# SwiGLU half steps by seven products of quarters: sums of products kept in PSUM chains, and operand sums moved from GpSimd to VectorE

## The chip, the cores and the metric

The kernel runs on one core of one Trainium2 chip. The metric is the device time of one execution in microseconds (us). The engines are called TensorE (PE in the rows; PEld is its weight load), VectorE (DVE), ScalarE (ACT), GpSimd (POOL) and SyncE (SP, which issues the DMAs here).

## What is computed

One step of a hybrid block for 128 prompt tokens and 512 sample tokens: a SwiGLU half step, a mixer (a gated delta rule and attention), a second SwiGLU half step, and the final norm. D_MODEL is 1024, D_FF is 2816. The change concerns the two half steps:

```python
def modulate(x, shift, scale):
    return x * (1 + scale) + shift

def swiglu(h, w13, w2):
    a, b = jnp.split(h @ w13, 2, axis=-1)
    return (jax.nn.silu(a) * b) @ w2

def ffn_sublayer(x, norm_w, shift, scale, gate, w13, w2):
    return x + HALF_STEP * gate * swiglu(modulate(rms_norm(x, norm_w), shift, scale), w13, w2)

xp = ffn_sublayer(xp, norm_ffn1[l], sh1p, sc1p, g1p, ffn1_w13[l], ffn1_w2[l])
...
xs = ffn_sublayer(xs, norm_ffn1[l], sh1s, sc1s, g1s, ffn1_w13[l], ffn1_w2[l])
```

## The kernel before

Features lie on the 128 partitions and the 640 tokens (prompt and samples together) on the free axis, in two halves of 320. Every product is made from exact parts of float32 operands (a first part and a rest, called hi and lo), by three matmuls: hi x hi, hi x lo, lo x hi. `parts` makes them: ScalarE casts the hi part (L128: wh for 1024 columns, sh for 512), VectorE subtracts it for the lo part (L132: wl, sl). The weights come by DMA into three buffers called wraw.

A half step (`ffn`, L475) walks over 22 feature tiles of 128 in rounds of 4, 4, 3, 3, 4 and 4; after each round the projection with w2 adds the round's tiles to the residual. The first three tiles are direct products (`product`, L144), whose silu(a) * b is made at L491 and L492 (tile s). The other 19 of each half step, 38 in the kernel, are pairs (`product_pair`, L567): a and b of one feature tile, each split into quarters (two halves of k by two halves of the tokens), are made by seven products P1 to P7 instead of eight, by Winograd's form of Strassen's algorithm. A product of quarters is 12 matmuls of 128x128 by 128x320 (`products`, L200, matmul in L207).

For this the operands are combined. `combined_operands` (L527) sums the hi and lo parts of the token quarters on GpSimd (L536, 12 for each half step), makes T1, T2 and T3 from them on VectorE (L541) and splits them again (L545 on VectorE). `last_operand` (L550) does the same for T4: 8 sums on GpSimd (L558), then VectorE (L562, L564). In every pair, GpSimd makes four sums of weights f[0] to f[3] (L577 to L580, tile ss, four buffers), which `parts` splits. The end of the direct products and the first pairs are called a transition below; in the profiled execution they lie at 51 to 99 us and 1158 to 1203 us.

In a pair the seven products go in the order P1, P6, P5, P7, P2, P3, P4. Each of P1, P6, P5, P7 and P4 has a PSUM bank of its own out of a ring of four (aux), P2 and P3 share a tile of two banks (big, a ring of two). ScalarE copies P1 (L590). Then VectorE adds and multiplies:

```python
        nc.vector.tensor_tensor(u[:, 0], s[:, 0], p6, op=ALU.add)
...
        nc.vector.tensor_tensor(u[:, 0], u[:, 0], p7, op=ALU.add)
        nc.vector.tensor_tensor(u[:, 1], s[:, 1], p7, op=ALU.add)
...
        nc.vector.tensor_tensor(s, s, both[:, :, 0:HT], op=ALU.add)
        nc.scalar.activation(s, s, AF.Silu)
...
        nc.vector.tensor_tensor(s[:, 1], s[:, 1], u[:, 1], op=ALU.mult)
        nc.vector.tensor_tensor(u[:, 0], u[:, 0], p4, op=ALU.add)
        nc.vector.tensor_tensor(s[:, 0], s[:, 0], u[:, 0], op=ALU.mult)
```

They stand at L593, L596, L599, L600, L604 (both banks of big, 640 columns), L605 (silu, 640 columns), L608, L609 and L610. At the end of each tile ScalarE casts the result (gh, L501) and VectorE makes its rest (gl, L502). The order of the instructions on each engine is set by a scheduler from the order of the program, its priorities and the buffers; each engine then runs its queue in order.

Of the kernel before, what the change touches and what calls it, by code (L numbers as in the profile page):

```python
# [10 lines left out]
F32 = mybir.dt.float32  # L11
# [3 lines left out]
AF = mybir.ActivationFunctionType  # L15
# [4 lines left out]
P = 128  # L20
# [75 lines left out]
# columns of a half (0: the prompt and the first 192 samples, 1: samples alone) by kind, 0 prompt, 1 sample  # L96
# [3 lines left out]
class Net:  # L100
# [9 lines left out]
    # ---------------------------------------------------------------- weights  # L110
# [8 lines left out]
    def parts(self, raw, small=False):  # L119
        """Exact split of float32 weights into two float32r parts."""  # L120
# [23 lines left out]
    def product(self, w, xs, c0=0, split=None):  # L144
        """[128 features, tokens] = w^T x over the k tiles; operands come as exact parts. split: None for one
        view of both halves, otherwise a view of each half, in small tiles when true."""
# [38 lines left out]
    def products_by_half(self, ws, xs, done):  # L185
        """Several products with the second halves of all before the first ones; done(i, half, psum)."""
# [13 lines left out]
    def products(self, ps, w, xs):  # L200
        """One half of the tokens and of the k tiles: ps (+)= w^T x."""
        nc = self.nc
        wh, wl = w
        n = len(xs)
        for k, (xh, xl) in enumerate(xs):
            for j, (wt, xt) in enumerate(((wh, xh), (wh, xl), (wl, xh))):
                nc.tensor.matmul(  # L207
                    ps,
                    lhsT=wt[:, k * P : (k + 1) * P],
                    rhs=xt,  # L210
                    start=(k == 0 and j == 0),
                    stop=(k == n - 1 and j == 2),
                )

    # ---------------------------------------------------------------- small helpers
    def rsqrt(self, y, x):
        """y = x ** -0.5, elementwise on a small tile."""
# [14 lines left out]
    # ---------------------------------------------------------------- setup  # L232
# [37 lines left out]
    def modulation(self, m):  # L270
        """One of the nine modulation vectors, features on partitions, for prompt and sample; a generator with one
        quarter of the k tiles in each step."""
# [34 lines left out]
    def modulation_part(self, m0, g):  # L307
        """Two feature tiles (2 g, 2 g + 1) of the modulation vectors m0 and m0 + 1."""
# [35 lines left out]
    def scale_columns(self, m, at, t, d0=0, n=KD):  # L344
        """norm weight * (1 + scale) as per-partition columns."""
# [9 lines left out]
    def token_rstd(self, ss):  # L355
        """[128 tokens, n] sums of squares -> rstd."""
# [8 lines left out]
    def half_rstd(self, acc, h):  # L365
        """rstd of the tokens of one half, from squares [128, 2, 320]: columns of 128 tokens that start at 0, 128
        and 192, so the last one overlaps."""
# [8 lines left out]
    def half_rows(self, columns):  # L376
        """(column of 128 tokens, first token, tokens, place) -> a row [320] on each partition."""
# [19 lines left out]
    def modulated(self, hs, X, rb, A, m_shift, h, ds):  # L397
        """x * rstd * A + shift of one half as two exact parts, for the feature tiles ds."""
# [23 lines left out]
    def next_operands(self, last, X, A, m_shift):  # L422
        """Operands of the next products; last: the generator that makes the last tiles of X."""
# [14 lines left out]
    def add_square(self, acc, x, first):  # L438
        """acc (+)= x * x for one half."""
# [15 lines left out]
    def residual(self, ws, xs, X, gate, tail, weight=None):  # L455
        """X += gate * product, with the squares of the sums gathered in acc; the last tiles go by halves."""
# [18 lines left out]
    # ---------------------------------------------------------------- ffn  # L475
    def ffn(self, hs, X, gate, w13, w2, gpool, between=None, first=(), weight=None):
        """X += gate * swiglu(h); squares of the result are gathered into acc."""
# [49 lines left out]
    def combined_operands(self, hs):  # L527
        """The parts of the sums of quarters of h = [[B11, B12], [B21, B22]] (k halves by token halves) that
        product_pair takes: T1 = B12 - B11, T2 = B22 - T1, T3 = B22 - B12."""
        nc = self.nc  # L530
        T = [[], [], []]
        for d in range(KH):
            v = []
            for k, h in ((d, 1), (d, 0), (d + KH, 1)):
                t = self.tile(self.phase, [P, HT], F32, "ht", self.nht)
                nc.gpsimd.tensor_tensor(t, *(x[:, h, :].bitcast(F32) for x in hs[k]), op=ALU.add)  # L536
# [13 lines left out]
    def last_operand(self, hs, B):  # L550
        """B21 - T2, in the place of B12."""
        nc = self.nc
        B["T4"] = []
        for d in range(KH):
            v = []
            for x in (B["21"][d], B["T2"][d]):
                t = self.tile(self.phase, [P, HT], F32, "ht", self.nht)
                nc.gpsimd.tensor_tensor(t, x[0].bitcast(F32), x[1].bitcast(F32), op=ALU.add)  # L558
# [8 lines left out]
    def product_pair(self, w, ca, cb, B, s):  # L567
        """s = silu(a) * b for the products a, b of two tiles of features with h, by seven products of quarters
        in place of eight (Winograd's form of Strassen's product)."""
# [13 lines left out]
        for i in (1, 0, 2, 3):  # L583
            S[i] = self.parts(f[i], True)
        b22 = self.parts(b[:, n:], True)
        u = self.tile(self.phase, [P, 2, HT], F32, "u", self.nu)
        bank = lambda: self.aux_tile()[:, 0:HT]
        p1 = bank()
        self.products(p1, (ha[:, :n], la[:, :n]), B["11"])
        nc.scalar.copy(s[:, 0], p1)  # L590
        p6 = bank()
        self.products(p6, S[1], B["T2"])
        nc.vector.tensor_tensor(u[:, 0], s[:, 0], p6, op=ALU.add)  # L593
        p5 = bank()
        self.products(p5, S[0], B["T1"])
        nc.vector.tensor_tensor(s[:, 1], u[:, 0], p5, op=ALU.add)  # L596
        p7 = bank()
        self.products(p7, S[2], B["T3"])
        nc.vector.tensor_tensor(u[:, 0], u[:, 0], p7, op=ALU.add)  # L599
        nc.vector.tensor_tensor(u[:, 1], s[:, 1], p7, op=ALU.add)  # L600
        both = self.tile(self.big, [P, 2, 512], F32, "big", 2)
        self.products(both[:, 0, 0:HT], (ha[:, n:], la[:, n:]), B["21"])
        self.products(both[:, 1, 0:HT], S[3], B["22"])
# [1007 lines left out]
```

## Time and profile before

| | |
|---|---|
| three runs | 1602.48, 1606.65, 1610.18 us (median 1606.65) |
| profiled execution, span from first to last instruction | 1605.0 us (no time of its own is listed beside the span) |
| TensorE busy | 1542.7 us (96%) |
| VectorE busy | 1100.8 us (69%) |
| ScalarE busy | 664.5 us (41%) |
| GpSimd busy | 368.7 us (23%) |
| mean granted TensorE clock | 0.989 of full speed |
| first half step, mixer, second half step, output | about 51 to 500, 500 to 1137, 1137 to 1588, 1588 to 1605 us |

The busy share of an engine is an average over stages with different limits. The lists of waits name for each engine what it waited for last, and the timeline shows single instructions with their start and duration. A matmul's duration (0.31 us) is longer than the step from one to the next, as matmuls overlap in the engine.

### The profile page before, as it was taken

Reading aid. Unit: us, or ns where it says so; the run is one execution under the profiler, and the core shown is the slowest. Engines: PE = TensorE matmul, PEld = TensorE weight load, DVE = VectorE, ACT = ScalarE, POOL = GpSimd, SP = SyncE. Lnnn points to the kernel's source line nnn. Section 1 sums busy time; section 2 is a strip of 40 time slices with the busy share of each in tenths; the row PEclk is TensorE's granted clock in tenths of the full one; section 3 lists DMA queues with packets and bytes.
Section 4 is the critical chain, followed back from the end, with each engine's and each line's share of the span. In section 5 each row is a group of like instructions: output and inputs, shape, how many; then the busy total and the mean of one; then the engine's idle time right before and its main releaser. Section 6 shows DMA issues by size and latency. Waiting matters only on the chain.

```text
span 1605.0 us, 28532 instructions
## 1 busy us (share of the span) xinstructions
PE 1542.7 (96%) x11242; PEld 1457.5 (91%) x11242; DVE 1100.8 (69%) x2241; ACT 664.5 (41%) x1234; POOL 368.7 (23%) x306
## 2 busy tenths in 40 slices
PE   6989999999999899999899999999879999999998
PEld 4889999999999798788899999899879999999997
DVE  5866666668576768886665655764796766767675
ACT  4433323324243646554455544333542424334244
POOL 3632131222220220100221213000352232331310
PEclk8999999999999999999999999999999999999999
DMA  9444434545325241214533324545022322323122
GB/s 329 148 144 141 159 123 143 163 152 168 119 82 137 82 138 44 65 40 134 161 117 94 98 78 127 158 127 167 14 79 79 92 66 66 106 66 106 53 79 66
DMA packets 221296, 181.17 MB, mean 113 GB/s; under 512 B 16160, under 2 KB 198621, under 8 KB 221163
## 3 DMA queue, kind: packets, MB, share of 16 engines
q1 hardware_dynamic: 220907, 179.29, 36.3%
q8 instruction: 89, 1.46, 0.4%
q14 instruction: 44, 0.36, 0.1%
q0 software_dynamic: 256, 0.06, 0.0%
HBM read 161.59 MB, written 16.42 MB: 111 GB/s over the span
## 4 chain that ended last, share of the span: by engine, by line
PE 80%; DVE 11%; issue 3%; ACT 2%; DMA 2%; POOL 2%; SPq 0%; POOLq 0%; DVEq 0%; ACTq 0%
PE big L177 29%; PE aux L207 20%; PE aux L177 9%; PE aux L164 9%; PE big L207 8%; DVE ht L404 1%; DVE wl L132 1%; PE aux L281 1%; DVE ht L541 1%; DVE sl L132 1%; PE aux L161 1%; DMA wraw<-ffn_w 1%; DVE x L451 1%; DVE tl L545 1%; DVE cacc L867 1%
## 5 line engine op out<-in xcount | busy, mean ns | idle before, releaser
L128 ACT CAST wh<-wraw 128x1024 fp32r<-128x1024 f32 (+1 forms) x147 | 150.8, 1026 | 266.3 <-PE aux L177 90.1
L132 DVE TENSOR_TENSOR wl<-wraw,wh 128x1024 fp32r<-128x1024 f32 (+1 forms) x145 | 181.8, 1254 | 85.7 <-ACT wh L128 84.4
L177 PE MATMUL big<-hl,wh 128*128 128x320 f32 x768 | 194.7, 321 | 6.9 <-POOL hl L411 4.3
L177 PE MATMUL big<-hh,wh 128*128 128x320 f32 x768 | 187.8, 319 | 4.0 <-ACT hh L1293 1.8
L177 PE MATMUL big<-hh,wl 128*128 128x320 f32 x768 | 187.8, 315 | 0.7 <-DVE wl L132 0.7
L128 ACT CAST sh<-ss 128x512 fp32r<-128x512 f32 x152 | 92.5, 620 | 185.1 <-POOL ss L578 93.6
L577 POOL TENSOR_TENSOR ss<-wraw 128x512 f32<-128x512 f32 x38 | 53.9, 1418 | 485.0 <-DMA wraw<-ffn_w 337.3
L132 DVE TENSOR_TENSOR sl<-ss,sh 128x512 fp32r<-128x512 f32 x152 | 132.3, 880 | 46.8 <-ACT sh L128 45.9
L207 PE MATMUL aux<-th,sh 128*128 128x320 f32 x456 | 141.3, 310 | 3.2 <-DVE s L492 2.8
L177 PEld LDWEIGHTS big<-hl,wh 128*128 128x128 f32 x768 | 131.4, 190 | 13.0 <-POOL hl L411 7.0
L207 PE MATMUL aux<-tl,sh 128*128 128x320 f32 x456 | 141.1, 309 | 0.0
L207 PE MATMUL aux<-th,sl 128*128 128x320 f32 x456 | 140.8, 309 | 0.0
L177 PEld LDWEIGHTS big<-hh,wh 128*128 128x128 f32 x768 | 129.0, 190 | 9.8 <-issue 3.1
L177 PEld LDWEIGHTS big<-hh,wl 128*128 128x128 f32 x768 | 131.1, 190 | 5.8 <-issue 4.6
L451 DVE SCALAR_TENSOR_TENSOR x<-big,gate,x 128x128 f32<-128x128 f32 (+2 forms) x181 | 67.4, 422 | 34.6 <-PE big L177 34.3
L177 PE MATMUL big<-gh,wh 128*128 128x320 f32 x352 | 88.7, 313 | 1.1 <-ACT gh L501 1.1
L207 PEld LDWEIGHTS aux<-th,sh 128*128 128x128 f32 x456 | 85.8, 188 | 4.0 <-DVE s L492 3.0
L177 PE MATMUL big<-gl,wh 128*128 128x320 f32 x352 | 87.6, 310 | 0.0
L177 PE MATMUL big<-gh,wl 128*128 128x320 f32 x352 | 87.0, 308 | 0.0
L207 PEld LDWEIGHTS aux<-tl,sh 128*128 128x128 f32 x456 | 85.7, 188 | 0.0
L207 PEld LDWEIGHTS aux<-th,sl 128*128 128x128 f32 x456 | 85.7, 188 | 0.0
L1055 DVE TENSOR_TENSOR P<-aux,lv 128x512 f16<-128x512 f32 x70 | 48.2, 688 | 49.1 <-PE aux L164 49.1
(373 smaller groups left out, 4014.0 us busy)
## 6 DMA issues: line engine op xcount, KB each, us to landing
wraw<-ffn_w SPq DMA_DIRECT2D x116, 512.0 KB, 3.9
araw<-ada_w SPq DMA_DIRECT2D x56, 512.0 KB, 5.8
wraw<-w_in SPq DMA_DIRECT2D x35, 512.0 KB, 3.8
araw<-ada_w SPq DMA_DIRECT2D x32, 256.0 KB, 6.5
wraw<-ffn_w SPq DMA_DIRECT2D x16, 384.0 KB, 3.1
gd<-stage SPq DMA_DIRECT2D x16, 320.0 KB, 2.9
wraw<-w_out SPq DMA_DIRECT2D x8, 512.0 KB, 4.3
xd<-x SPq DMA_DIRECT2D x8, 320.0 KB, 2.2
```

Of the source, the lines that this page charges most:

```text
L128: nc.scalar.copy(hi, raw)
L132: nc.vector.tensor_sub(lo, raw, hi.bitcast(F32))
L161: self.marks.append(self.nc.tensor.transpose(*args))
L164: self.marks.append(self.nc.tensor.matmul(*args, **kw))
L177: self.nc.tensor.matmul(ps[h], lhsT=wt[:, k, c0 : c0 + P], rhs=xt[:, h, :], start=(k == 0 and j == 0), stop=(k == len(xs) - 1 and j == 2),)
L207: nc.tensor.matmul(ps, lhsT=wt[:, k * P : (k + 1) * P], rhs=xt, start=(k == 0 and j == 0), stop=(k == n - 1 and j == 2),)
L281: nc.tensor.matmul(ps[32 * g : 32 * g + 32], lhsT=self.s32[:, k, :], rhs=raw[:, g * 256 : (g + 1) * 256], start=(k % 2 == 0), stop=(k % 2 ...
L404: mark = nc.vector.scalar_tensor_tensor(t[:, cols], X[d][:, h, cols], A[:, d, v : v + 1], rb[:, cols], op0=ALU.mult, op1=ALU.mult)
L451: nc.vector.scalar_tensor_tensor(X[:, h, cols], ps[:, cols], gate[:, d, v : v + 1], X[:, h, cols], op0=ALU.mult, op1=ALU.add)
L541: nc.vector.tensor_sub(f[i], v[x], v[y] if y < 3 else f[0])
L577: nc.gpsimd.tensor_tensor(f[0], b[:, :n], b[:, n:], op=ALU.add)
L1055: nc.vector.tensor_tensor(P16, p1, mask, op=ALU.mult)
```

## The change

`products` gets an argument `start`; without it, the product is added to what its bank holds. In `product_pair` the products go in the order P1, P5, P6, P3, P7, P2, P4. P1, P6, P7 and P4 add up in one bank (`chain`, the first of a big tile), P5 and P3 in another (`side`, an aux bank); P2 has the second bank of the big tile. ScalarE copies the chain after P1 (c1), the side after P5 (c5) and the chain after P6 (c6); VectorE makes five operations instead of eight, and the silu goes by halves. The weight sums are split in the order 0, 1, 3, 2. The sums of L536 and L558 go to VectorE. Lines of the changed kernel behind `products` are one higher than before; the changed line numbers of the pair are L593, L596, L599 (the copies c1, c5, c6), L601 (s1), L603 (c5 + chain), L604 (silu), L606 (s0), L608, L609 (silu) and L610. The diff also takes out comments, which are left out here.

```diff
-    def products(self, ps, w, xs):
+    def products(self, ps, w, xs, start=True):
...
-                    start=(k == 0 and j == 0),
+                    start=(start and k == 0 and j == 0),
                     stop=(k == n - 1 and j == 2),
+                    skip_group_check=not start,
...
     def combined_operands(self, hs):
...
-                nc.gpsimd.tensor_tensor(t, *(x[:, h, :].bitcast(F32) for x in hs[k]), op=ALU.add)
+                nc.vector.tensor_tensor(t, *(x[:, h, :].bitcast(F32) for x in hs[k]), op=ALU.add)
...
     def last_operand(self, hs, B):
...
-                nc.gpsimd.tensor_tensor(t, x[0].bitcast(F32), x[1].bitcast(F32), op=ALU.add)
+                nc.vector.tensor_tensor(t, x[0].bitcast(F32), x[1].bitcast(F32), op=ALU.add)
...
     def product_pair(self, w, ca, cb, B, s):
...
-        for i in (1, 0, 2, 3):
+        for i in (0, 1, 3, 2):
             S[i] = self.parts(f[i], True)
         b22 = self.parts(b[:, n:], True)
-        u = self.tile(self.phase, [P, 2, HT], F32, "u", self.nu)
-        bank = lambda: self.aux_tile()[:, 0:HT]
-        p1 = bank()
-        self.products(p1, (ha[:, :n], la[:, :n]), B["11"])
-        nc.scalar.copy(s[:, 0], p1)
-        p6 = bank()
-        self.products(p6, S[1], B["T2"])
-        nc.vector.tensor_tensor(u[:, 0], s[:, 0], p6, op=ALU.add)
-        p5 = bank()
-        self.products(p5, S[0], B["T1"])
-        nc.vector.tensor_tensor(s[:, 1], u[:, 0], p5, op=ALU.add)
-        p7 = bank()
-        self.products(p7, S[2], B["T3"])
-        nc.vector.tensor_tensor(u[:, 0], u[:, 0], p7, op=ALU.add)
-        nc.vector.tensor_tensor(u[:, 1], s[:, 1], p7, op=ALU.add)
         both = self.tile(self.big, [P, 2, 512], F32, "big", 2)
-        self.products(both[:, 0, 0:HT], (ha[:, n:], la[:, n:]), B["21"])
-        self.products(both[:, 1, 0:HT], S[3], B["22"])
-        nc.vector.tensor_tensor(s, s, both[:, :, 0:HT], op=ALU.add)
-        nc.scalar.activation(s, s, AF.Silu)
-        p4 = bank()
-        self.products(p4, b22, B["T4"])
-        nc.vector.tensor_tensor(s[:, 1], s[:, 1], u[:, 1], op=ALU.mult)
-        nc.vector.tensor_tensor(u[:, 0], u[:, 0], p4, op=ALU.add)
-        nc.vector.tensor_tensor(s[:, 0], s[:, 0], u[:, 0], op=ALU.mult)
+        chain, p2 = both[:, 0, 0:HT], both[:, 1, 0:HT]
+        side = self.aux_tile()[:, 0:HT]
+        kept = lambda: self.tile(self.phase, [P, HT], F32, "ht", self.nht)
+        self.products(chain, (ha[:, :n], la[:, :n]), B["11"])
+        c1 = kept()
+        nc.scalar.copy(c1, chain)
+        self.products(side, S[0], B["T1"])
+        c5 = kept()
+        nc.scalar.copy(c5, side)
+        self.products(chain, S[1], B["T2"], start=False)
+        c6 = kept()
+        nc.scalar.copy(c6, chain)
+        self.products(side, S[3], B["22"], start=False)
+        nc.vector.tensor_tensor(s[:, 1], c6, side, op=ALU.add)
+        self.products(chain, S[2], B["T3"], start=False)
+        nc.vector.tensor_tensor(c5, c5, chain, op=ALU.add)
+        nc.scalar.activation(s[:, 1], s[:, 1], AF.Silu)
+        self.products(p2, (ha[:, n:], la[:, n:]), B["21"])
+        nc.vector.tensor_tensor(s[:, 0], c1, p2, op=ALU.add)
+        self.products(chain, b22, B["T4"], start=False)
+        nc.vector.tensor_tensor(s[:, 1], s[:, 1], c5, op=ALU.mult)
+        nc.scalar.activation(s[:, 0], s[:, 0], AF.Silu)
+        nc.vector.tensor_tensor(s[:, 0], s[:, 0], chain, op=ALU.mult)
```

The change also moves instructions. Three places matter; the names are tiles, with a number of their buffer or version.

On TensorE, in a pair of the fifth round of the second half step, before: the end of P7 (its own bank, aux) and the start of P2 (big).

```order
L207 MATMUL aux_16538<-th_13510,sh_16483 128x320
L207 MATMUL aux_16538<-tl_13511,sh_16483 128x320
L207 MATMUL aux_16538<-th_13510,sl_16484 128x320
L207 MATMUL big_16553<-hh_12512,wh_16471 128x320 [waits PE_49]
L207 MATMUL big_16553<-hl_12513,wh_16471 128x320
L207 MATMUL big_16553<-hh_12512,wl_16472 128x320
```

The same place after the change: the end of P7 (the chain in big_16431), five matmuls of the next pair's P1 (big_16573), and the start of P2, which is in the tile of the chain.

```order
L207 MATMUL big_16431<-tl_13473,sh_16423 128x320
L207 MATMUL big_16431<-th_13472,sl_16424 128x320
L207 MATMUL big_16573<-hh_12466,wh_16549 128x320 [waits DVE_49]
L207 MATMUL big_16573<-hl_12467,wh_16549 128x320
L207 MATMUL big_16573<-hh_12466,wl_16550 128x320
L207 MATMUL big_16573<-hh_12468,wh_16549 128x320
L207 MATMUL big_16573<-hl_12469,wh_16549 128x320
L207 MATMUL big_16431<-hh_12474,wh_16407 128x320 [waits DVE_49]
L207 MATMUL big_16431<-hl_12475,wh_16407 128x320
```

P2 followed P7 directly and waited for no reader of P7. Now five matmuls of the next P1 stand between, and P2 waits for VectorE: for L603, which reads the chain. P4 stands in the same way behind L606 and five more such matmuls.

On ScalarE, in the second pair of that round, before: the copy of P1 (L590), casts of the pair before (gh) and of the weight sums (sh), and the cast of a weight that is being loaded for the pair after the next (wh).

```order
L590 COPY s_16314<-aux_16352 128x320
L501 CAST gh_16168<-s_16170 128x320
L128 CAST sh_16475<-ss_16464 128x512
L128 CAST wh_16615<-wraw_16603 128x1024
L128 CAST sh_16479<-ss_16463 128x512
L128 CAST sh_16483<-ss_16465 128x512
L128 CAST sh_16487<-ss_16466 128x512
```

The same place after the change, with the copies c1 (L593), c5 (L596) and c6 (L599).

```order
L593 COPY ht_16303<-big_16289 128x320
L502 CAST gh_16108<-s_16110 128x320
L128 CAST wh_16549<-wraw_16537 128x1024
L128 CAST sh_16411<-ss_16399 128x512
L596 COPY ht_16317<-aux_16290 128x320
L128 CAST sh_16415<-ss_16400 128x512
L599 COPY ht_16331<-big_16289 128x320
L128 CAST sh_16419<-ss_16402 128x512
```

The cast wh stood behind the only copy of the pair. Now it stands ahead of c5 and c6, for which the products P3 and P7 wait.

On VectorE, at the start of the first half step's transition, before: the first operations on the combined operands (ht, tl) and on two weights (wl).

```order
L132 TENSOR_TENSOR wl_659<-wraw_656,wh_658 128x1024
L541 TENSOR_TENSOR ht_777<-ht_771,ht_773 128x320
L541 TENSOR_TENSOR ht_779<-ht_775,ht_771 128x320
L132 TENSOR_TENSOR wl_714<-wraw_711,wh_713 128x1024
L541 TENSOR_TENSOR ht_781<-ht_775,ht_777 128x320
L545 TENSOR_TENSOR tl_784<-ht_777,th_783 128x320
```

The same place after the change.

```order
L537 TENSOR_TENSOR ht_771<-hh_209,hl_210 128x320
L537 TENSOR_TENSOR ht_773<-hh_209,hl_210 128x320
L132 TENSOR_TENSOR wl_659<-wraw_656,wh_658 128x1024
L537 TENSOR_TENSOR ht_775<-hh_217,hl_218 128x320
L132 TENSOR_TENSOR wl_714<-wraw_711,wh_713 128x1024
L542 TENSOR_TENSOR ht_777<-ht_771,ht_773 128x320
L542 TENSOR_TENSOR ht_779<-ht_775,ht_771 128x320
L542 TENSOR_TENSOR ht_781<-ht_775,ht_777 128x320
L546 TENSOR_TENSOR tl_784<-ht_777,th_783 128x320
```

The sums of the hi and lo parts (L537, GpSimd's L536 before) now stand in VectorE's own queue ahead of the differences of L542 (L541 before) that take them.

## Rows read from the trace of the kernel before

**Rows 1.** The page, its first part: busy us, share of the span, number of instructions of each engine.

```profile
PE 1542.7 (96%) x11242; PEld 1457.5 (91%) x11242; DVE 1100.8 (69%) x2241; ACT 664.5 (41%) x1234; POOL 368.7 (23%) x306
```

**Rows 2.** By stretch: length, busy PE, PEld, DVE, ACT, POOL; granted clock, DMA share, GB/s.

```profile
51.00:99.00 48.00, 40.23 (x281) 36.74 (x284) 40.90 (x56) 19.11 (x38) 32.18 (x25) 0.93 0.43 143
1158.00:1203.00 45.00, 36.94 (x237) 36.09 (x236) 43.22 (x55) 21.26 (x41) 28.71 (x25) 0.92 0.23 71
...
1210.00:1400.00 190.00, 190.00 (x1293) 189.34 (x1292) 132.78 (x234) 68.90 (x109) 56.31 (x40) 1.00 0.27 81
```

**Rows 3.** What TensorE waited for: line and what released it, us, times, longest.

```profile
PE aux L177 <- DVE s L492: 5.9, 1, 5.9
...
PE aux L207 <- DVE wl L132: 4.6, 1, 4.6
...
PE aux L207 <- DVE s L492: 2.8, 1, 2.8
```

**Rows 4.** The same view by stretch as rows 2, behind two long waits of TensorE.

```profile
89.00:95.50 6.50, 6.42 (x27) 6.42 (x28) 6.04 (x12) 4.08 (x9) 0.35 (x1) 0.58 0.41 126
1193.90:1197.00 3.10, 3.10 (x13) 3.10 (x13) 3.10 (x5) 0.62 (x2) 1.42 (x2) 0.51 0.53 169
```

**Rows 5.** TensorE in order of time: start, duration; first and last matmul of a P1.

```profile
1445.20 0.31 PE L207 MATMUL aux<-hh,wh 128*128 128x320 f32 x1
...
1446.81 0.31 PE L207 MATMUL aux<-hh,wl 128*128 128x320 f32 x1
```

**Rows 6.** Groups by line and shape: busy us, mean ns | idle before, releaser.

```profile
L541 DVE TENSOR_TENSOR ht<-ht,ht 128x320 f32<-128x320 f32 x24 | 20.7, 906 | 4.5 <-POOL ht L536 4.5
L545 DVE TENSOR_TENSOR tl<-ht,th 128x320 fp32r<-128x320 f32 x24 | 20.4, 874 | 0.1
L593 DVE TENSOR_TENSOR u<-s,aux 128x320 f32<-128x320 f32 x38 | 18.4, 485 | 27.5 <-PE aux L207 26.8 <-ACT s L590 0.6
```

**Rows 7.** VectorE and GpSimd in order of time in the first half step's transition.

```profile
66.91 1.97 DVE L541 TENSOR_TENSOR ht<-ht,ht 128x320 f32<-128x320 f32 x3 [1.28 <-POOL ht L536]
68.80 3.35 DVE L545 TENSOR_TENSOR tl<-ht,th 128x320 fp32r<-128x320 f32 x3
...
68.55 3.24 POOL L536 TENSOR_TENSOR ht<-hh,hl 128x320 f32<-128x320 f32 x3 [0.84 <-DVE ht L541]
```

**Rows 8.** VectorE, ScalarE and GpSimd in order of time around one pair.

```profile
1454.77 0.47 DVE L599 TENSOR_TENSOR u<-u,aux 128x320 f32<-128x320 f32 x1
1455.16 0.47 DVE L600 TENSOR_TENSOR u<-s,aux 128x320 f32<-128x320 f32 x1
...
1447.16 0.43 ACT L590 COPY s<-aux 128x320 f32<-128x320 f32 x1 [0.85 <-PE aux L207]
...
1450.84 1.05 ACT L128 CAST wh<-wraw 128x1024 fp32r<-128x1024 f32 x1 [1.40 <-DMA wraw<-ffn_w]
1451.79 1.17 ACT L128 CAST sh<-ss 128x512 fp32r<-128x512 f32 x2
...
1445.48 1.49 POOL L580 TENSOR_TENSOR ss<-wraw,ss 128x512 f32<-128x512 f32 x1 [0.69 <-DVE sl L132]
```

**Rows 9.** Groups by line and shape as in rows 6.

```profile
L608 DVE TENSOR_TENSOR s<-s,u 128x320 f32<-128x320 f32 x38 | 21.6, 569 | 7.8 <-ACT s L605 7.8
...
L590 ACT COPY s<-aux 128x320 f32<-128x320 f32 x38 | 16.2, 426 | 36.1 <-PE aux L207 28.5 <-DVE gl L502 7.6
```

**Rows 10.** VectorE, then TensorE in order of time, end of a wait for L492.

```profile
1200.76 0.88 DVE L492 TENSOR_TENSOR s<-s,aux 128x320 f32<-128x320 f32 x2
...
1201.30 0.42 PE L207 MATMUL aux<-th,sh 128*128 128x320 f32 x1 [2.75 <-DVE s L492]
1201.55 0.31 PE L207 MATMUL aux<-tl,sh 128*128 128x320 f32 x1
```

**Rows 11.** The page, its sixth part: DMA issues, KB each, us from issue to landing.

```profile
wraw<-ffn_w SPq DMA_DIRECT2D x116, 512.0 KB, 3.9
```

**Rows 12.** The instructions of L608: least, median and largest duration in ns.

```profile
L608 DVE TENSOR_TENSOR s<-s,u x38: 478/492/1519, 112.6 to 1559.9; 128x320 f32<-128x320 f32 x38
```

## The prediction

> **What bounds the kernel now.** I read the profile from the whole to the part. The busy shares come first: TensorE is busy for 96% of the span and nobody else for more than 69% [rows 1], so the time can only change where TensorE's work changes or where it waits. The number of matmuls doesn't change. The windows by stage come next [rows 2]: through the steady part of the second half step TensorE is busy for 190.0 of 190 us at full clock, while around the two transitions (direct products to products of quarters) it is busy for only 40.2 of 48 and 36.9 of 45 us, at a mean clock of 0.93 and 0.92. There VectorE is busy for 40.9 of 48 and 43.2 of 45 us and GpSimd for 32.2 and 28.7 us. Then TensorE's list of waits [rows 3] names those stalls: 5.9 us and 2.8 us for an s of L492, 4.6 us for a wl. After the two long ones it runs at half clock, 1.2 GHz: 27 matmuls in 6.5 us and 13 in 3.1 us [rows 4]. At full clock 11 steps of a product take 1.61 us, so one takes 0.147 us [rows 5]; the half clock has cost 6.5 - 27 x 0.147 = 2.5 and 3.1 - 13 x 0.147 = 1.2 us. All that can come back is therefore 5.9 + 2.5 = **8.4 us** in the first half step and 4.6 + 2.8 + 1.2 = **8.6 us** in the second. In the 38 pairs there is nothing to win, since TensorE doesn't wait in them, but something to lose.
>
> **The sums that move to VectorE (gain).** The 24 additions of L541 take 0.906 us and the 24 of L545 0.874 us, although the same shape with an operand in PSUM (L593) takes 0.485 us [rows 6]. The timeline shows why: they run long beside GpSimd's L536 and come to an end with it [rows 7]. The Trainium skill (SBUF — State Buffer, section "Who interferes with whom") says that a VectorE instruction with two SBUF inputs and a GpSimd one that reads SBUF exclude each other for a whole instruction; by that rule, the trace agrees. The excess of the two groups is 24 x 0.42 + 24 x 0.39 = 19.5 us, about 9.7 in each half step, and VectorE also waits 4.5 us for L536. What is added is 20 sums in each half step, one every 0.40 us (a 0.47 to 0.49 us instruction starts 0.39 us before the next one, L599 to L600 [rows 8]): 8.0 us. In the first half step VectorE has 7 of 48 us idle besides, mostly waits for GpSimd, so the late s comes early enough: I take all **8.4 us**, and none if its queue is still late. In the second it is idle for under 2 of 45 us, the net relief is some 2 us in these two groups and perhaps 5 more in the sl, wl and gl that GpSimd held up too: I take **6.4** of 8.6, with bounds 1 and 8.6. Sum: -14.8 us (bounds -1 and -17).
>
> **The chains (loss).** Before, each product had its own PSUM bank, and its reader could be late without harm: in the pair shown P7, the fourth product, ended near 1445.20 + 47 x 0.147 + 0.31 = 1452.4, and L599 read it at 1454.77 [rows 5, 8]. Now four products go to one tile, and the next matmul on it waits until it was read. The removed VectorE work (8 additions and multiplications a pair down to 5) and the two more copies and one more silu on ScalarE (a copy is 0.43 us [rows 9]) lie beside TensorE; I cost them at nothing while those queues keep up.
>
> 1. P2 waits for VectorE's L603 and P4 for L606, each with five matmuls of another product before it. From the start of the last matmul of P7 the fillers give 6 x 0.147 = 0.88 us. The way round needs 0.31 (the matmul) + 0.04 (end of a matmul at 1447.12 to the copy at 1447.16 [rows 5, 8]) + 0.48 (the addition) + 0.06 (an s that ends at 1201.24 to the matmul at 1201.30 [rows 10]) = 0.89 us. It comes 0.01 us late, and after any wait the second matmul starts 0.25 instead of 0.147 us behind the first [rows 10], so each costs 0.115 us. For 38 pairs: 2 x 38 x 0.115 = **8.7 us** (bounds 0, if five matmuls are just enough, and 12). The Trainium skill (PSUM — Partial Sum Buffer, section "PSUM bank collisions raise a hardware error") asks for such guards by bank. P2 writes another bank than the one that L603 reads; by that rule its wait wouldn't be needed and the sum would be 4.4 us lower. The program's order has the wait, as the tile of two banks is guarded as one, so I keep 8.7.
>
> 2. ScalarE works in order, and the cast of a weight that must first be loaded (wh) now stands ahead of the copy c5. In the pair shown wh began at 1450.84, after 1.40 us of waiting for its load; the load follows GpSimd's last sum of the pair before, which ended at 1446.97, by 3.9 us [rows 8, 11]. P1 began at 1445.20, so P3, which needs c5, is due 36 x 0.147 = 5.3 us later, at 1450.5. c5 would come behind wh (0.95) and one sh (0.52): 1450.84 + 0.95 + 0.52 + 0.43 + 0.06 = 1452.8, 2.3 us late. GpSimd's sum had waited 0.69 us for an sl [rows 8], which the shorter VectorE queue may give back: I take 1.6. The next pair is itself later by that and I take 1.1 there; the first and last pair of a round have no such load ahead: 2.7 us for each of three rounds of four pairs. In the two rounds of three the wh of the projection stands ahead of c1 instead; without the sh it is 1.8 late by the same rows, and I take 1.6. Second half step: 3 x 2.7 + 2 x 1.6 = **11.3 us** (bounds 0, if loads start earlier, and 3 x 4.6 + 2 x 1.8 = 17).
>
> 3. In the first half step wh stands ahead of c1 or of no copy in most pairs: **2 us** (0 to 10).
>
> 4. VectorE's L608, ahead of the L606 that P4 needs, takes 0.492 us in the median but up to 1.519 us beside GpSimd, 0.09 us over its least on average (0.569 against 0.478 [rows 9, 12]): 38 x 0.09 = **3.4 us** (0 to 16, below).
>
> Loss: 8.7 + 11.3 + 2 + 3.4 = 25.4 us. Sum: 1605.0 - 14.8 + 25.4 = 1615.6 us against the profiled execution, whose span is 1605.0 us. The median of the three runs is 1606.65, 1.65 us more: **1617 us**. The mixer keeps its order and counts for nothing.
>
> **The rivals.**
> - *The bridges hold, faster.* Five matmuls are just enough and the loads come early, since the load chain hangs on GpSimd, which has lost 40 sums. What is left of the loss is some 3 us; all 17 us come back: 1606.65 - 17 + 3 = 1593 us. For it: the way round misses by only 0.01 us. Against it: the wait of 1.40 us for a load [rows 8] is there although GpSimd had long been idle. It decides at the point where c5 ends before 36 matmuls of its pair have gone.
> - *Only the loads cost, same.* Bridges hold (-8.7) and the rest stays: 1617 - 9 = 1608 us.
> - *GpSimd's sums fall into the round trips, slower still.* If they meet L608 or the gl behind it in half of the pairs, for the 1.0 us that the worst L608 shows, the loss grows by 19 x 1.0 - 3.4 = 16: 1633 us. The skill's rule on exclusion, named above, makes this the worst case for each pair. Against it: the median L608 isn't slowed [rows 12].
> - *VectorE is still late at the transitions.* The 40 sums that it takes on cost 16 us of its time, nearly as much as the 19.5 us won. Then only some 4 of the 14.8 us come back: 1628 us.
>
> **How the numbers follow.** Forecast 0.38 (1617, own range 1609 to 1625). Bridges hold 0.23 (1593). Only the loads 0.20 (1608). GpSimd in the round trips 0.09, VectorE late 0.10. The measurement tells 0.5%, about 8 us, from no change: under 1598.6 is faster, over 1614.7 slower. Faster: 0.23 and a little of the second rival, 0.26. Slower: two thirds of the forecast, 0.25, and both late cases, 0.19, together 0.44. Same: the rest, 0.30. The range leaves out the lower half of the first rival and the end of the late cases: 1593 to 1632 us.
>
> **What would show it.** Right: the waits for s of L492 and for wl at the transitions are gone and the clock there is near 1.0; in the pairs new waits appear on TensorE for L603 and L606 of some 0.1 us each and for copies c1 and c5 of 1 to 2 us in the middle pairs of a round, with ScalarE waiting for a load ahead. Wrong: no wait over 0.3 us within the pairs (the first rival), or stalls at the transitions as long as before, or clock lost in the steady stretch, which nothing above counts.

## The result and the profile after

The changed kernel takes 1634.77 us in the median of its executions, the kernel before 1606.65 us: the ratio is 1.0165, with an interval of 1.0145 to 1.0184. The prediction was 1617 us with a range to 1632, so the direction was right and the size was not: by the ratio 27 us were lost where 10 were forecast. One execution, of 3283.83 us, in which the matmuls of pairs took some 0.55 us each in place of 0.31, is left out of the ratio, and its cause is open. The profile below is that of a later execution of the same kernel (the first experiment).

The first part of the page, which answers to [rows 1], and the windows, which answer to [rows 2]:

```profile
PE 1562.3 (96%) x11242; PEld 1459.7 (90%) x11242; DVE 1061.3 (65%) x2167; ACT 696.0 (43%) x1348; POOL 336.1 (21%) x266
```

```profile
51.00:99.00 48.00, 44.45 (x332) 40.61 (x331) 39.20 (x77) 20.04 (x42) 8.72 (x4) 1.00 0.54 170
1158.00:1203.00 45.00, 40.05 (x256) 38.72 (x255) 41.39 (x88) 26.92 (x57) 10.27 (x8) 0.96 0.18 53
...
1210.00:1400.00 190.00, 183.81 (x1230) 180.42 (x1230) 122.38 (x197) 69.66 (x123) 59.09 (x40) 1.00 0.26 77
```

TensorE has the same number of matmuls and the span is 25 us longer. TensorE's busy time is 20 us longer too (1542.7 before), so much of the loss lies in matmuls that take longer, and no list of waits shows that part. In the window of the first transition it is busy for 44.5 instead of 40.2 us, in that of the second for 40.1 instead of 36.9, and the granted clock there rose from 0.93 and 0.92 to 1.00 and 0.96. GpSimd has fallen from 32.2 to 8.7 us. So the transitions have won, as forecast. The steady stretch, in which TensorE was busy for all of 190 us, now has 183.8.

TensorE's list of waits, which answers to [rows 3]:

```profile
PE big L207 <- DVE s L606: 13.5, 13, 2.5
...
PE aux L177 <- DVE wl L132: 3.7, 1, 3.7
PE big L207 <- ACT ht L593: 3.6, 7, 1.3
...
PE aux L207 <- ACT ht L596: 0.6, 1, 0.6
```

The waits of 5.9 and 2.8 us for s are gone; one of 3.7 us for a wl is left at the second transition. New are 13.5 us in 13 places for L606, the addition that P4 waits for, and 4.2 us for the copies c1 (L593) and c5 (L596). One pair of the second half step, on VectorE, ScalarE, GpSimd and TensorE in order of time (start, duration):

```profile
1251.78 0.49 DVE L603 TENSOR_TENSOR ht<-ht,big 128x320 f32<-128x320 f32 x1
1252.34 1.22 DVE L132 TENSOR_TENSOR sl<-ss,sh 128x512 fp32r<-128x512 f32 x1
1253.49 0.48 DVE L608 TENSOR_TENSOR s<-s,ht 128x320 f32<-128x320 f32 x1
1254.49 0.98 DVE L503 TENSOR_TENSOR gl<-s,gh 128x320 fp32r<-128x320 f32 x1 [0.52 <-ACT gh L502]
1255.39 0.48 DVE L606 TENSOR_TENSOR s<-ht,big 128x320 f32<-128x320 f32 x1
```

```profile
1254.00 0.46 ACT L502 CAST gh<-s 128x320 fp32r<-128x320 f32 x1 [1.69 <-DVE s L608]
```

```profile
1251.72 1.29 POOL L580 TENSOR_TENSOR ss<-wraw,wraw 128x512 f32<-128x512 f32 x1 [0.63 <-DVE sl L132]
1253.71 1.42 POOL L581 TENSOR_TENSOR ss<-wraw,ss 128x512 f32<-128x512 f32 x1 [0.69 <-DVE sl L132]
```

```profile
1252.32 0.42 PE L207 MATMUL big<-hh,wh 128*128 128x320 f32 x1
1252.58 0.32 PE L207 MATMUL big<-hl,wh 128*128 128x320 f32 x1
...
1254.06 0.46 PE L207 MATMUL big<-hh,wl 128*128 128x320 f32 x2
...
1255.92 0.41 PE L207 MATMUL big<-hh,sh 128*128 128x320 f32 x1 [0.83 <-DVE s L606]
```

P2 starts at 1252.32 and its last matmul at 1254.06, so L606 could have read it near 1254.4. It starts at 1255.39. Ahead of it in VectorE's queue stand an sl of 1.22 us, L608, and a gl that first waits for ScalarE's gh and then takes 0.98 us; sl and gl run beside two sums of GpSimd, and in the median of the trace they take 0.69 and 0.49 us. TensorE stands idle for 0.83 us ahead of P4 for that alone. P2's own wait, for L603, costs what the prediction said: its second matmul comes 0.26 us behind its first.

### The profile page after: what moved, and what is told of

It is laid out like the page before. It is cut to its first block, busy times and chain, and to the rows that moved or that the text cites. A ratio compares the mean times of both kernels' runs of the same rounds, so it can differ in the third digit from the quotient of the medians.

```text
span 3282.1 us, 28408 instructions
## 1 busy us (share of the span) xinstructions
PE 3266.0 (100%) x11242; PEld 2945.3 (90%) x11242; DVE 1019.2 (31%) x2167; ACT 708.5 (22%) x1348; POOL 302.9 (9%) x266
## 4 chain that ended last, share of the span: by engine, by line
PE 99%; DVE 0%; issue 0%; DMA 0%; ACT 0%; SPq 0%; DVEq 0%; ACTq 0%
PE big L177 38%; PE big L207 23%; PE aux L177 14%; PE aux L207 9%; PE aux L164 9%; PE aux L282 3%; PE aux L161 1%; PE aux L323 1%; PE aux L1344 0%; PE aux L1250 0%; PE aux L382 0%; PE aux L883 0%; PE aux L1239 0%; PE aux L372 0%; PE big L1396 0%
## 5 line engine op out<-in xcount | busy, mean ns | idle before, releaser
L177 PE MATMUL big<-hl,wh 128*128 128x320 f32 x768 | 334.7, 526 | 0.9 <-DVE hl L417 0.6
L177 PE MATMUL big<-hh,wl 128*128 128x320 f32 x768 | 327.5, 516 | 0.0
L177 PE MATMUL big<-hh,wh 128*128 128x320 f32 x768 | 326.9, 522 | 0.1
L177 PEld LDWEIGHTS big<-hh,wl 128*128 128x128 f32 x768 | 233.9, 319 | 15.0 <-issue 8.3
L177 PEld LDWEIGHTS big<-hh,wh 128*128 128x128 f32 x768 | 230.9, 317 | 17.5 <-issue 6.3
L177 PEld LDWEIGHTS big<-hl,wh 128*128 128x128 f32 x768 | 232.9, 319 | 10.9 <-issue 2.2
L207 PE MATMUL big<-th,sh 128*128 128x320 f32 x304 | 168.4, 554 | 0.0
L207 PE MATMUL big<-th,sl 128*128 128x320 f32 x304 | 168.3, 554 | 0.0
L207 PE MATMUL big<-hl,wh 128*128 128x320 f32 x304 | 167.8, 552 | 0.0
L207 PE MATMUL big<-tl,sh 128*128 128x320 f32 x304 | 167.6, 551 | 0.0
L177 PE MATMUL big<-gh,wl 128*128 128x320 f32 x352 | 166.3, 554 | 0.0
L207 PE MATMUL big<-hh,wl 128*128 128x320 f32 x304 | 165.2, 555 | 0.0
L207 PE MATMUL big<-hh,wh 128*128 128x320 f32 x304 | 164.9, 542 | 0.0
L207 PEld LDWEIGHTS big<-hh,wh 128*128 128x128 f32 x304 | 99.4, 327 | 34.4 <-issue 15.8
```

The source lines that it names most:

```text
L177: self.nc.tensor.matmul(ps[h], lhsT=wt[:, k, c0 : c0 + P], rhs=xt[:, h, :], start=(k == 0 and j == 0), stop=(k == len(xs) - 1 and j == 2),)
L207: nc.tensor.matmul(ps, lhsT=wt[:, k * P : (k + 1) * P], rhs=xt, start=(start and k == 0 and j == 0), stop=(k == n - 1 and j == 2), skip_gr ...
```

## The experiments

All times are compared with runs of the kernel before on the same chip; differences in us are made from the ratios and 1606.8 us. A ratio's interval is 2 to 5 us wide to either side, so differences of a few us between two runs aren't clear of noise.

**The change again.** No edit.

> The changed kernel itself, for a profile that can be read beside that of before and a second interval. Every theory expects 1630 to 1636 us, some 27 us more than before. The prediction's account (transitions win 15 us, waits in the pairs cost 25) must be off by 17 us somewhere: if the transitions didn't win, the stalls behind s of L492 (L493 now) and wl are still there with 4 us and more; if the pairs cost more, TensorE's new waits in the 38 pairs add up to some 42 us, and the list of waits says which of L603, L606 and the copies carry them.

Measured: 1635.79 us, ratio 1.0181 [1.0162, 1.0199]. The profile is the one above.

**The sums alone.** The kernel before, with the sums of L536 and L558 on VectorE:

```diff
-                nc.gpsimd.tensor_tensor(t, *(x[:, h, :].bitcast(F32) for x in hs[k]), op=ALU.add)
+                nc.vector.tensor_tensor(t, *(x[:, h, :].bitcast(F32) for x in hs[k]), op=ALU.add)
...
-                nc.gpsimd.tensor_tensor(t, x[0].bitcast(F32), x[1].bitcast(F32), op=ALU.add)
+                nc.vector.tensor_tensor(t, x[0].bitcast(F32), x[1].bitcast(F32), op=ALU.add)
```

> The kernel before with the sums of L536 and L558 on VectorE and nothing else. Theory A (the sums free VectorE of GpSimd, as in the prediction): 15 us faster than before, about 1592 us, with the long waits for s and wl at the two transitions gone. Theory B (VectorE is as late with the sums as without): within 4 us of before. Then the whole loss of 27 us is the chains'.

Measured: 1597.94 us, ratio 0.9942 [0.9921, 0.9963], 9 us faster than before (6 to 13 by the interval). That lies between the two theories. VectorE at the second transition, and what TensorE still waits for:

```profile
1171.14 1.29 DVE L536 TENSOR_TENSOR ht<-hh,hl 128x320 f32<-128x320 f32 x3
```

```profile
PE aux L207 <- DVE s L492: 3.4, 2, 2.0
...
PE aux L207 <- DVE sl L132: 2.1, 1, 2.1
```

Three sums end after 1.29 us, one every 0.40 us, as priced. The stalls at the transitions (13.3 us in [rows 3]) shrink to 5.5 us and don't vanish.

**The chains alone.** The change with the two lines of the last diff back on GpSimd.

> The changed kernel with the sums of L537 and L559 back on GpSimd. Theory A: 15 us slower than the change, about 1649 us, since the chains alone cost some 42 us. Theory B: about the time of the change, 1630 to 1638 us.

Measured: 1649.08 us, ratio 1.0267 [1.0242, 1.0293]: the chains cost 43 us alone, and beside them the sums win 14 us, as theory A had it. The intervals of this 14 and of the 9 us above overlap.

```profile
PE big L207 <- DVE s L606: 10.2, 13, 1.6
PE big L207 <- ACT ht L593: 8.0, 6, 3.3
PE aux L177 <- DVE s L493: 5.9, 1, 5.9
...
PE big L207 <- DVE wl L132: 3.9, 1, 3.9
```

The stalls of before (5.9 us for s, 3.9 us for wl) stand beside the new ones for L606 and the copies.

**P2 in a tile of its own.**

```diff
-        chain, p2 = both[:, 0, 0:HT], both[:, 1, 0:HT]
+        chain, p2 = both[:, 0, 0:HT], self.aux_tile()[:, 0:HT]
```

> The changed kernel with P2 in a tile of its own (a bank of aux) in place of the second bank of the chain's tile, so that neither P2 nor P4 waits for a reader of the other bank; P4 still waits for L603, with the 12 matmuls of P2 between. The prediction's term 1 (two round trips with five matmuls each, 0.115 us a wait): 8.7 us faster than the change, about 1625 us. If the round trips are the main loss (0.5 us and more a wait, VectorE late): 20 to 40 us faster than the change, 1595 to 1613 us. If the copies behind loads are the loss: within 5 us of the change.

Measured: 1620.75 us, ratio 1.0083 [1.0064, 1.0103], 16 us faster than the change. The wait for L606 has gone from the list, and another has grown:

```profile
PE big L207 <- ACT ht L593: 19.9, 13, 3.9
```

```profile
1454.31 1.04 ACT L128 CAST wh<-wraw 128x1024 fp32r<-128x1024 f32 x1 [4.35 <-DMA wraw<-ffn_w]
1455.27 0.42 ACT L593 COPY ht<-big 128x320 f32<-128x320 f32 x1
```

ScalarE waits 4.35 us for a loaded weight, and the copy c1 that P6 needs stands behind its cast; TensorE waits 3.9 us for it. In the change these waits were smaller (3.6 us in all), as TensorE had already waited for L606: the two waits cover each other, which the next run bears out. So the 16 us are not the 13.5 us of L606, which came back at c1. They are the price of the shared tile, and the run that keeps it (below) shows what it is made of.

**L608 held behind L606.**

```diff
-        nc.vector.tensor_tensor(s[:, 0], c1, p2, op=ALU.add)
+        s0 = nc.vector.tensor_tensor(s[:, 0], c1, p2, op=ALU.add)
...
-        nc.vector.tensor_tensor(s[:, 1], s[:, 1], c5, op=ALU.mult)
+        with self.tc.issue_after(s0.ins):
+            nc.vector.tensor_tensor(s[:, 1], s[:, 1], c5, op=ALU.mult)
```

> The change with one multiplication (L608, s1 times c5) held behind the addition L606 on VectorE, so that L606, which P4 waits for, doesn't stand behind L608 and the gl of the half before. If L608 and gl ahead of L606 are the cause of the 13.5 us that TensorE waited for L606: these waits go, 14 to 18 us faster than the change, 1616 to 1621 us. If they only covered the copies behind loads (as the run with P2 in its own tile suggests, where 19.9 us of waits for c1 appeared): the waits for c1 and c5 grow and the gain is 2 to 10 us, 1625 to 1633 us.

Measured: 1638.33 us, ratio 1.0193 [1.0167, 1.022], the time of the change within the intervals, and below the gain that even the second theory allowed.

```profile
PE big L207 <- ACT ht L593: 13.1, 8, 4.5
...
PE aux L207 <- ACT ht L596: 4.0, 4, 2.0
```

The 13.5 us for L606 are gone, though GpSimd's sums run as before: the place in VectorE's queue made L606 late, and GpSimd's sums alone don't. But 17.1 us for c1 and c5 have taken their place, against 4.2 in the change. Removing one of two waits that cover each other won nothing here.

**Casts of loaded weights held behind the copies.**

```diff
-            nc.scalar.copy(hi, raw)
+            with self.tc.issue_after(self.c6s[-2].ins) if len(self.c6s) > 1 and not small else ExitStack():
+                nc.scalar.copy(hi, raw)
...
-        nc.scalar.copy(c6, chain)
+        self.c6s.append(nc.scalar.copy(c6, chain))
```

> The change with every cast of a loaded weight (wh) held on ScalarE behind the copy c6 of the pair before last, so that no copy stands behind a cast that waits for a load. By the prediction's term 2 the copies cost 11.3 us: 1624 us. By the list of waits of the change they cost 4.2 us, and L606 stays: 1629 to 1632 us. If TensorE then only comes earlier to the wait for L606: no gain, 1633 to 1636 us. A loss would mean that the casts themselves come late.

Measured: 1644.46 us, ratio 1.022 [1.019, 1.0251], so no gain; the 6 us more than the change are within the intervals (lines of this kernel and the ones below it are one to three higher).

```profile
PE big L208 <- DVE s L607: 13.8, 13, 1.9
PE big L208 <- DVE ht L604: 12.6, 16, 1.8
...
PE big L208 <- ACT ht L594: 1.3, 1, 1.3
```

```profile
1272.43 0.49 DVE L602 TENSOR_TENSOR s<-ht,aux 128x320 f32<-128x320 f32 x1 [0.58 <-ACT wh L129]
1272.83 2.07 DVE L133 TENSOR_TENSOR wl<-wraw,wh 128x1024 fp32r<-128x1024 f32 x1
1274.83 1.75 DVE L133 TENSOR_TENSOR sl<-ss,sh 128x512 fp32r<-128x512 f32 x1
1276.50 0.47 DVE L604 TENSOR_TENSOR ht<-ht,big 128x320 f32<-128x320 f32 x1
```

The copies are in time (1.3 us left), but the later cast puts its rest wl right ahead of L604, the addition that P2 waits for: wl and an sl, which take 2.07 and 1.75 us beside GpSimd's sums (1.22 and 0.69 in the median), keep it from 1272.83 until 1276.50.

**Both: own tile and casts behind the copies.** The diffs of the two runs together.

> P2 in a tile of its own and the casts behind the copies, both at once. If waits on readers of the shared tile and copies behind loads are together the whole cost of the chains: TensorE doesn't wait in the pairs, and what is left is the win of the sums at the transitions, 1593 to 1600 us, like the run with the sums alone (1598) or better. If a third cost stands behind them: 1605 us or more, with its wait in the list.

Measured: 1605.33 us, ratio 0.9989 [0.9974, 1.0005]. One edit alone gave -16 us, the other +6 (within the intervals), together they give -31. The third cost is there too, the wait of P4 for L604, which still stands behind a wl:

```profile
PE big L208 <- DVE ht L604: 7.6, 9, 1.3
```

**The three together.** The last kernel with L608 behind L606.

> P2 in a tile of its own, the casts behind the copies, and L608 behind L606. P4 doesn't wait for L606 here, so the third part should do nothing: within 3 us of the run with the first two. If it is slower by more, holding L608 back delays the gh and gl that the projection needs.

Measured: 1607.88 us, ratio 0.9989 [0.9973, 1.0005]: the third edit does nothing here, as expected.

**Own tile, casts and rests behind.** The kernel with own tile and casts behind, and besides:

```diff
-                nc.vector.tensor_sub(lo, raw, hi.bitcast(F32))
+                with self.tc.issue_after(self.adds[-2].ins) if len(self.adds) > 1 and not small else ExitStack():
+                    nc.vector.tensor_sub(lo, raw, hi.bitcast(F32))
...
-        nc.vector.tensor_tensor(c5, c5, chain, op=ALU.add)
+        self.adds.append(nc.vector.tensor_tensor(c5, c5, chain, op=ALU.add))
```

> P2 in a tile of its own, the casts behind the copies, and besides VectorE's rest of each loaded weight (wl) held behind the addition c5 + chain of the pair before last. The run without the last part still waited 7.6 us, in 9 pairs, for that addition, which stood behind a wl of 1.84 us and an sl of 1.77 us slowed by GpSimd. If the place in VectorE's queue is the cause: these waits go and the time is 1594 to 1599 us, at or below the run with the sums alone. If GpSimd's sums slow sl enough by themselves: the waits stay at half, about 1601 us. If wl then comes late for the next P1: 1605 us or more, with wl in the list of waits.

Measured: 1595.12 us, ratio 0.9926 [0.9899, 0.9954]. This is faster than both kernels. The wait for the addition has left the list, and a steady window is nearly full again:

```profile
1205.00:1395.00 190.00, 189.44 (x1292) 189.18 (x1292) 124.42 (x204) 75.03 (x136) 56.14 (x38) 1.00 0.28 81
```

**The shared tile kept, the rest cleared.** The change with L608 behind L606, the casts behind c6, and wl behind L606 (`self.adds.append(s0)`).

> The change with the shared tile kept, and everything else taken out of the way of its two round trips: casts of loaded weights behind c6, their wl behind L606, L608 behind L606. What is left should be the round trips themselves, 2 x 38 waits of 0.115 us (8.7 us, the prediction's term 1), and the modulation's matmuls that the scheduler splits to fill them (9 us in the first half step by the profile of the change), less the 8 us that the sums win: 1614 to 1618 us. If 1630 us or more, the round trips cost several times what the prediction took for them, or another instruction has taken the place of those moved.

Measured: 1612.27 us, ratio 1.0032 [1.0017, 1.0046]. One pair's P2 on TensorE:

```profile
1259.46 0.41 PE L209 MATMUL big<-hh,wh 128*128 128x320 f32 x1
1259.71 0.31 PE L209 MATMUL big<-hl,wh 128*128 128x320 f32 x1
```

P2 starts in step and its second matmul comes 0.25 us later instead of 0.147, as the prediction's term 1 has it. In the second half step 19 such steps, at the start of P2, and 19 at the start of P4 lose 2.0 us each; term 1 has 4.4 us for that half. In the first half step there are some 25 more such steps than in the kernel with P2's own tile, about 2.5 us. But this kernel is still 17 us slower than the one with the tile of its own. Most of the rest is in the modulation's matmuls (L284 here, L281 before), which run in the first half step. The windows of that line alone, before, in the change, here, in the change with P2's own tile and nothing else, and in the run with the casts held behind the copies (busy TensorE, number):

```profile
51.00:494.20 443.20, 30.19 (x448) 11.61 (x448) 0.99 0.44 141
```

```profile
51.00:503.90 452.90, 39.58 (x448) 13.24 (x448) 1.00 0.44 138
```

```profile
51.00:495.00 444.00, 39.58 (x448) 13.24 (x448) 1.00 0.45 139
```

```profile
51.00:491.00 440.00, 30.63 (x448) 11.74 (x448) 1.00 0.44 142
```

```profile
51.00:509.30 458.30, 36.14 (x448) 12.68 (x448) 1.00 0.44 137
```

The same 448 small matmuls take 9.4 us more in the change and here. In the kernel before, and with P2's own tile, they come in 27 runs of 16 (and two of 8). In the change and here 15 of these runs are cut in two, since some of their matmuls serve as the fillers between P7 and P2 or between P2 and P4; with the casts held behind, 9 runs are cut and the matmuls take 6 us more. That is 0.6 to 0.7 us for a cut in all three. These 9.4 us and the two sums of short steps, 4.0 and 2.5, come to 16 of the 17 us.

**The cleared chains without the sums.** The fastest variant with the sums back on GpSimd.

> The fastest of the variants (P2 in its own tile, casts and rests of loaded weights held behind) with the sums of L537 and L559 back on GpSimd. If chains whose waits are all covered cost nothing, and the win of that variant is the sums' alone: the time of before within 0.5%, 1600 to 1612 us, with the waits for s of L493 and for wl at the transitions as in before. If the chains win something by themselves (VectorE has three operations fewer in a pair): below 1600 us. If the sums win 13 us beside chains and 8 without: about 1608 us.

Measured: 1609.55 us, ratio 1.0016 [1.0003, 1.0029].

```profile
PE aux L179 <- DVE s L495: 5.8, 1, 5.8
...
PE big L209 <- DVE wl L134: 3.9, 1, 3.9
...
PE big L209 <- ACT ht L595: 3.2, 2, 2.9
```

The waits at the transitions are those of before; of the new ones, 3.2 us for c1 are left. Chains cleared so far win nothing and cost 0 to 5 us, though VectorE has three operations fewer in each pair: TensorE bounds the pairs, not VectorE. The sums win 14.5 us beside them (some 10 to 19 by the intervals).

## Why the prediction was wrong

The variants make a ladder from before to the change, in us against before: cleared chains without the sums +3, with them -12, with the shared tile +5, with the scheduler's own places for L608 and the loaded weights +29 (the first measurement of the change gives +27). A rung is uncertain by 4 to 5 us. The rung of the shared tile also moves two holds (the rests go behind L606 instead of L603, and L608 is held); the one edit of P2's tile alone gives 16 us for it. Each rung answers to a part of the sum.

- **The sums.** Forecast -14.8, measured -14.5 on the cleared chains, -14 from the chains alone to the change, and -9 on the kernel before, which isn't clear of the other two by the intervals. The size and the mechanism (VectorE freed from GpSimd) were right for the kernel that was forecast; the second transition keeps a stall of 3.7 us, where the forecast had left 2.2 us.
- **Term 1, the round trips.** Forecast 8.7. The steps themselves are about right (4.0 and 2.5 us in the two half steps against 4.4 each). The step that failed is that the five filler matmuls were costed at nothing, as matmuls that have to run anyway. In the first half step many are taken out of runs of the modulation's matmuls, and cutting these runs costs 9.4 us. The rung of the shared tile is 17 us. The Trainium skill (PSUM — Partial Sum Buffer, section "PSUM bank collisions raise a hardware error") asks for guards by bank, and the prediction put 4.4 us on that rule, for P2's wait. By that rule P4's wait for L606 isn't needed either, since L606 reads the bank of P2 and P4 writes that of the chain, so both round trips, 8.7 us in the forecast's prices, hung on it. P2 in a tile of its own frees both: 16 us alone, 17 in the ladder.
- **Terms 2 to 4, the queues.** Forecast 11.3 + 2 + 3.4 = 16.7 us, measured 24 us as one rung. The split was wrong: the copies c1 and c5 cost 4.2 us of waiting instead of 13, and L606 13.5 instead of 3.4. Term 4 took the mean slowdown of L608 alone, 0.09 us; ahead of L606 stand L608 itself, the gl behind it with its wait for gh, and an sl beside GpSimd. Term 4 is the second step that failed: a queue was priced by the slowdown of one instruction and not by all that stands ahead of the reader. The loads that term 2 named are there, and show at once when L606 is made early (17.1 us). The terms were added as if each wait were its own; in the change they overlap, and so taking one away won nothing. The list of waits has 17.7 of the 24 us. An estimate of the rest: each of its 21 waits costs 0.27 us more than the list counts (it counts from the modelled end of the last matmul, 0.31 us behind its start, where a step is 0.147, and the second matmul behind a wait comes 0.25 us after the first), 5.6 us; and behind the longest wait, of 2.5 us until 1399.5, the granted clock is at half, 1.2 GHz, for 3.4 us (row below), in which 12 matmuls run that take 1.8 us in step, so that 1.6 us are lost. Together these make up the rung. Clock lost within the pairs is one of the prediction's own signs of being wrong.
- **The rivals.** "GpSimd's sums fall into the round trips" gave 1633 us, close to the time, and its place (L608 and the gl behind it) was right. Its cause was only half of it: with L606 ahead of L608 the wait goes while GpSimd's sums stay. And it has nothing for the 9.4 us of the fillers, so that its number lies so near is in part luck. "The bridges hold" was wrong: with the queues cleared and the tile shared, each round trip still costs its 0.1 us, the fillers 9.4 us, and the time is 1612. The fastest variant comes near that rival's 1593 us, but it has no bridges, as P2 has a tile of its own.
- In sum: -14.8 for the sums was right; the chains were forecast at 25.4 us and cost 43: 9 us more for the fillers, 7 more for the queues, and some 3 (0 to 5) for the chains with most waits cleared, whose cause is open, less 2 for the round trips. The range ended at 1632, two or three us short; a price of 9 us on the fillers would have taken its end past the measured time.

The window of the change at half clock (length, busy TensorE; the granted clock is the 0.50):

```profile
1399.40:1402.80 3.40, 3.29 (x12) 3.30 (x13) 0.05 (x1) 0.47 (x1) 0.78 (x1) 0.50 0.38 112
```

## What to carry to other kernels

When an addition moves from an engine into a chain in PSUM, every reader between two products of the chain comes onto TensorE's path: list what stands ahead of each reader in its queue, up to what that itself waits for, before counting the reader's own time. List too what the scheduler can put between two products of a chain: here matmuls of another kind cost 0.6 us for each run that was cut to put them there. The tile of two banks was guarded as one here, so give a product that isn't in the chain its own tile. Where two waits cover each other, test their removal together: here clearing L606 alone gave +2 us and clearing the copies alone +6, neither clear of noise, and clearing both, with the rests of the loaded weights, gave -24.

## What the runs showed of the hardware

Small matmuls of 128x32 run four at a time, and cutting a run of them breaks up these rounds of four. The TensorE timeline of before, with a whole run of 16:

```profile
156.40 1.07 PE L281 MATMUL aux<-araw,s 128*32 128x256 f32 x16
157.40 0.41 PE L207 MATMUL aux<-hh,wh 128*128 128x320 f32 x1
```

The same in the change, with a run cut into 10 and 6:

```profile
144.18 1.05 PE L282 MATMUL aux<-araw,s 128*32 128x256 f32 x10
145.16 0.41 PE L207 MATMUL big<-hh,wh 128*128 128x320 f32 x1
...
147.11 0.63 PE L282 MATMUL aux<-araw,s 128*32 128x256 f32 x6
147.68 0.41 PE L207 MATMUL big<-hh,wh 128*128 128x320 f32 x1
```

From the first start to the next large matmul the whole run takes 1.00 us (156.40 to 157.40), the piece of 10 takes 0.98 us (144.18 to 145.16) and the piece of 6 takes 0.57 us (147.11 to 147.68). So 10 matmuls take as long as 16. The starts of the single matmuls in the trace tell why. In the whole run they come in rounds of 4, 4, 4 and 4, the four of a round within 0.02 us and one round about 0.22 us behind the other. In the pieces the rounds are 4, 4, 1, 1 and 3, 3, and a round of one takes as long as a round of four. The windows in which only the last round still runs show its size, in the whole run and in the piece of 10 (the number in the first brackets counts them):

```profile
157.26:157.38 0.12, 0.12 (x4) 0.00 (x0) 1.00 0.56 166
```

```profile
145.05:145.15 0.10, 0.10 (x1) 0.00 (x0) 1.00 0.00 0
```

All 448 small matmuls make 112 rounds before and 142 in the change, two more for each of the 15 cuts. At 0.22 us these 30 rounds are 6.6 of the 9.4 us. The rest is the way into and out of one more run for each cut: 0.24 us from a large matmul to the first small one, where a step between large ones takes 0.147, and 0.31 us from the last small one to the next large one, where a round takes 0.22. That is some 0.2 us for each cut. The Trainium skill (TensorEngine Tiling (Array Packing), section "Key Properties") says that changing the tiling mode drains TensorE; the trace agrees as far as these 0.2 us go, and no run here separates the drain from other delays.
